# Scoring two blocks of keys during attention instead of during the projections, in a two-layer decoder trunk

## The chip, the cores and the metric

The kernel runs on one core of a Trainium2 chip, as one launch. The metric is the device time of that core in microseconds (us). The time of the kernel before is the median of three runs; one further execution was taken with the hardware profiler.

## The reference, cut to what matters

Two layers over 1024 tokens of width 1024, float32. The change lies in the token mixer of layer 0, a sparse attention: a small "indexer" scores all keys for each query, the 256 best keys that lie before the query are kept, and attention with 16 heads (4 groups) sees only these. `proj` holds q, k, v, the index queries `qi` (8 heads of 64), one index key `ki`, and the 8 head weights `wi`.

```python
def block_fn(args):                      # one block of 128 queries
    qb, qib, wib, start = args
    s = jnp.einsum('bqhd,bsd->bqhs', qib, ki)
    score = jnp.einsum('bqhs,bqh->bqs', jax.nn.relu(s), wib)
    score = jnp.where(causal[None], score, -jnp.inf)
    _, sel = lax.top_k(score, topk)      # topk = 256
    ...
    logits = jnp.where(sel_ok[:, :, None, None, :], logits, -1e30)
    p = jax.nn.softmax(logits, axis=-1)
    o = jnp.einsum('bqgrk,bqkgd->bqgrd', p, vg)
```

After it follow the output projection, a dense FFN, and in layer 1 a short convolution and another FFN; they fill the time from about 640 us to the end and are not touched.

## The kernel before, in words

**A planner writes the order.** The program first records all operations with a due time (`plan.pri`), and `Plan.drain` then plays them through with the costs of `Plan.cost` and issues, for each engine, the ready operation with the earliest due time. So each engine gets a fixed order; an operation with a late due time is pulled forward where the planner finds its engine free. Due times are only an order: attention's run behind the real clock. Block b's attention has due times from `t_att[b]` to `t_att[b+1]`; worked out from lines 829 to 831 `t_att` is 280.6, 287.4, 301.0, 321.4, 348.6, 390.5, 440.7, 499.4 and 566.4 for b = 0 to 8.

**Buffers are rings, in the order in which they are recorded.** `Pool.tile` gives a tile of a ring only after the tile before it has been given, and after all uses of the one `bufs` places back have been issued, whatever the due times are:

```python
if len(ring) > 1:
    plan.link(ring[-2].alloc, al)
if len(ring) > bufs:
    old = ring[-1 - bufs]
    for o in old.ops:
        plan.link(o, al)
```

Two rings matter here: `s4` (SBUF, 3 tiles of 128x1024, shown as `s` in the trace), used by the scoring and by the end of each selection; and `ps_L` (PSUM, 2 tiles), used by every product of `pair_products`: the scoring's and attention's own q k.

**Projections** (`project`). ki is projected first, then the index queries in four steps (half of the tokens, half of the heads), each of two weight tiles (`rope_pair`), rotated and stored to DRAM (`qid`). Then k, q and v.

**Scoring** (`index`). For block b the index queries are loaded back (`karena<-qid`), and for four pairs of heads TensorE multiplies them with the index keys (`ps_L<-karena`, (b+1)*128 columns, at most 512 at a time), ScalarE applies Relu into an `s4` tile, and VectorE multiplies with the head weight and adds (`sc<-s,wiT`). Blocks 0 and 1 need none.

**Counting** (`select`). For a pair of blocks the 256th largest score is found by 31 steps of a binary search on its bits. A step counts, for both blocks, the scores above a threshold, on ScalarE with Sign and an accumulator (pairs 2/3 and 6/7) or on VectorE (pair 4/5) (`junk<-sc,bs`), and then updates the threshold with three small VectorE operations (`bs<-bs`). The due times of the steps go evenly from that of the record to `self.until`. **The end** (`selected`): some ten VectorE passes over `s4` tiles per block, which write `bias`, the mask that attention adds.

**Attention** (`attend`). For each block, group and pair of heads: q k into `ps_L`, mask and maximum on VectorE (`p<-ps_L,bias`), Exp on ScalarE (`p<-p,nm,qsc`), transposes on TensorE, copies to SBUF (`pf<-ps`, ScalarE, or VectorE where the planner finds it free sooner), products with v (`ps_o<-pf,vst`). During blocks 4 and 5 the output projection of the first half (`out_tile`) runs as well. The attention's pools open when the projections' pools (`hp`, `pj`) have been drained.

Of the kernel before, what the change touches and what calls it, by code (L numbers as in the profile page):

```python
# [9 lines left out]
F32 = mybir.dt.float32  # L10
# [40 lines left out]
class Store:  # L51


    def __init__(self, space):
        self.space, self.real, self.parts, self.ops = space, None, {}, []
        self.alloc, self.closed = None, False
# [394 lines left out]
P = 128  # L451
# [3 lines left out]
TB = T // P  # L455
# [6 lines left out]
IH = 8  # L462
TOPK = min(256, T // 4)
FREE_BLK = TOPK // P
# [14 lines left out]
def half_of(h):  # L479
    return slice(h * HW, (h + 1) * HW)  # L480


def blk(b):
    return slice(b * P, (b + 1) * P)
# [313 lines left out]
class Attention:  # L798
# [3 lines left out]
    def __init__(self, tk, w, w_out, ada_w, xspill):  # L802
        self.tk, self.nc, self.w, self.w_out = tk, tk.nc, w, w_out
        self.plan = plan = tk.plan
        self.ada_w, self.xspill = ada_w, xspill

        def dram(name, shape):
            return plan.wrap(plan.tc.dram_tile(shape, F32, name=name), shape)

        self.qd = dram("qd", [HEADS * HD, T])  # L810
        self.qid = dram("qid", [IH * HD, T])
        self.kd = dram("kd", [KVH * HD, T])
        self.rd = dram("rd", [2, 4, 32, T // 4])
        self.kp = Pool(plan, "k4")
        self.keep = keep = Pool(plan, "keep", side="right")
        self.sel = sel = Pool(plan, "sel", side="right")
        self.hp = Pool(plan, "h", side="right")
        self.pj = Pool(plan, "pj", bufs=2, rt=5)
        self.op = Pool(plan, "o", side="right")
        self.at = Pool(plan, "at", bufs=2)  # L820
        self.bias = [keep.tile([P, (b + 1) * P], BF16, name="bias%d" % b) for b in range(TB)]
        self.ssq = keep.tile([P, TB, HEADS], F32, name="ssq")
        self.qsc = keep.tile([P, TB, HEADS], F32, name="qsc")
        self.qsn = keep.tile([P, TB, HEADS], F32, name="qsn")
        self.score = [None] * FREE_BLK + [sel.tile([P, (b + 1) * P], F32, name="sc%d" % b)
                                          for b in range(FREE_BLK, TB)]
        self.bs = sel.tile([P, 4, 16], F32, name="bs")
        self.junk = [sel.tile([P, n], BF16, name="junk%d" % n) for n in (6 * P, T)]
        cum = np.cumsum([0] + [6.8 * (b + 1) for b in range(TB)])
        w = np.array([0.0] * 5 + [41.0 / 26 * (c / 6.8 - 10) for c in cum[5:]])  # L830
        self.t_att = self.T_PROJ + 38 * self.SLOT + cum + w
        self.until = {2: self.t_att[2], 4: self.t_att[4] + 10.0, 6: self.t_att[7]}

    def arena(self, i):

# [75 lines left out]
    def project(self):  # L911
        tk, nc, sp, plan = self.tk, self.nc, self.pj, self.plan
        self.kist = self.arena(0)
        self.ssk = sp.tile([P, TB, KVH], F32, name="ssk", bufs=1)
        self.wiT = sp.tile([P, TB, IH], F32, name="wiT", bufs=1)
        s = 0
        self.unit(s)
        n = HD + IH
        kw = self.s4()
        self.plan.pri = 26.0  # L920
        w = tk.wcols(self.w, C_KI, n)
        for half in range(NH):
            self.unit(s)
            nc.scalar.copy(kw[0:n, half_of(half)], tk.gemm_tile(w, n, self.h[half]))
            s += 1
        self.unit(s + 1)
        self.ki_chain(kw)
        ends = []
        for half, j in ((0, 0), (0, 1), (1, 1), (1, 0)):
            self.unit(s)  # L930
            if (half, j) != (1, 1):
                w = tk.wpair(self.w, C_QI + j * 2 * P)
            ts = slice(max(0, FREE_BLK * P - half * HW), HW)
            ab, sl, e = self.rope_pair(w, half, ts, None, None, s)
            s += (e - s) * (ts.stop - ts.start) / HW
            for two in range(2):
                self.to_dram(ab[two], self.qid, j, two, half, sl)
            if (half, j) == (0, 1):
                ends += self.indexed(s, (2, 3))
        self.free_bias()  # L940
        ends += self.indexed(s, (4, 5, 6, 7))
        for pri, end, args in sorted(ends, key=lambda e: e[0]):
            plan.pri = pri
            end(*args)
        self.unit(s)
        w = tk.wpair(self.w, C_K)
        for half in range(NH):
            ab, sl, s = self.rope_pair(w, half, slice(0, HW), 1, self.ssk, s)
            rk = sp.tile([P, 4, KVH], F32, name="rk", tag="rk")
            tk.rsqrt_small(rk.rearrange("p a b -> p (a b)"),  # L950
                           self.ssk[:, half * 4:half * 4 + 4].rearrange("p a b -> p (a b)"),
                           1.0 / HD, sp.tile([P, 64], F32, name="rst", tag="rst8"))
            self.k_out(ab, rk, half, sl)
        self.load_k()
        for j in range(HEADS // 4):
            self.unit(s)
            w = tk.wpair(self.w, j * 2 * P)
            for half in range(NH):
                ab, sl, s = self.rope_pair(w, half, slice(0, HW), 0,
                                           self.ssq[:, :, 4 * j:4 * j + 4], s)  # L960
                for two in range(2):
                    self.to_dram(ab[two], self.qd, j, two, half, sl)
        self.unit(s)
        tk.rsqrt_small(self.qsc.rearrange("p a b -> p (a b)"),
                       self.ssq.rearrange("p a b -> p (a b)"), 1.0 / HD,
                       sp.tile([P, HW], F32, name="rst", tag="t2"),
                       mult=float(HD ** -0.5))
        nc.vector.tensor_scalar(self.qsn, self.qsc, -1.0, None, op0=ALU.mult)
        w = [tk.weights(tk.cols(self.w[half_of(i)], C_V, KVH * HD)) for i in range(2)]
        for b in range(TB):  # L970
            ps = tk.ps()[:, 0:KVH * HD]
            for k in range(KT):
                hi, lo = (v[:, blk(b % 4)] for v in self.h[b // 4](k))
                tk.mm3(ps, hi, lo, *w[k // 4](k % 4), k == 0, k == KT - 1)
            plan.copy(self.vst.part_of(b)[:, b], ps)
            s += 0.5
            self.unit(s)

    def indexed(self, t, blocks):

# [221 lines left out]
    def attend(self):  # L1202
        tk, nc, plan = self.tk, self.nc, self.plan
        self.o, self.banks, tail = [], 0, None
        self.steps = [(layer, j, i, k) for layer, j in ((0, 2), (0, 3), (0, 4), (0, 5), (1, 0))
                      for i in range(NH) for k in range(KT)]
        for b in range(TB):
            if b % 2 == 0:
                self.o.append([self.op.tile([P, KT, 2 * P], F32R, name="o%s%d" % (v, b),
                                            tag="o" + v, bufs=3) for v in ("hi", "lo")])  # L1210
# [691 lines left out]
```

## Time and profile before

| | us |
|---|---|
| median of 3 runs | 2338.97 (2336.26 to 2341.29) |
| profiled execution, its own time | 2337.17 |
| its span, first to last instruction | 2335.5 |
| TensorE busy in the span | 2259.2 (97%) |
| VectorE, ScalarE busy | 1808.3 (77%), 1115.1 (48%) |

All times in the rows are us from the start of the span. PE is TensorE's matmuls, PEld its weight loads, DVE VectorE, ACT ScalarE, SP the queue that issues the DMAs. In a row of instructions an entry in brackets is the idle time of the engine before it, and what ended it. Every operation is recorded by one helper, so all have the line L244; the tiles tell them apart.

### The profile page before, as it was taken

The numbers are of one execution on the slowest core, as the hardware profiler recorded it, in microseconds if no ns is written. First come the engines' busy times: TensorE is split into PE (matmuls) and PEld (weight loads), VectorE is DVE, ScalarE is ACT, GpSimd is POOL, SyncE is SP. The second block draws the span as 40 slices with busy tenths as digits, with TensorE's granted clock in tenths as the row PEclk, the third lists the DMA queues.
The fourth block names the chain that finished last, engine by engine and source line by source line (L and its number), as shares of the span: only waits on it lengthen the run. The fifth ranks groups of instructions, "written<-read, shape, count | busy, mean of one in ns | idle before, by whom it ended". The sixth has DMA issues, their size and how long they took to land.

```text
span 2335.5 us, 32751 instructions
## 1 busy us (share of the span) xinstructions
PE 2259.2 (97%) x11742; PEld 1827.0 (78%) x11742; DVE 1808.3 (77%) x3697; ACT 1115.1 (48%) x2125; POOL 5.6 (0%) x19
## 2 busy tenths in 40 slices
PE   6999999999999999999999899999999999999999
PEld 6667876877797878888788778878877888887887
DVE  6879999777689886767599899976788655555995
ACT  3576899746655333333344552234553333333443
POOL 0000000000000000000000000000000000000000
PEclk7999999999999999999999999999999999999999
DMA  8423233443344543444845134225344322337443
GB/s 285 136 64 91 90 118 101 140 127 96 109 129 138 182 152 123 151 138 151 302 146 179 57 111 135 82 90 171 104 122 140 91 86 90 100 119 281 141 167 113
DMA packets 305132, 312.30 MB, mean 134 GB/s; under 512 B 15145, under 2 KB 209738, under 8 KB 304970
## 3 DMA queue, kind: packets, MB, share of 16 engines
q1 hardware_dynamic: 303530, 308.91, 41.6%
q8 instruction: 92, 1.51, 0.3%
q10 hardware_dynamic: 1440, 1.31, 0.2%
q14 instruction: 70, 0.57, 0.1%
HBM read 259.05 MB, written 51.12 MB: 133 GB/s over the span
## 4 chain that ended last, share of the span: by engine, by line
PE 71%; DVE 13%; issue 7%; DMA 6%; ACT 3%; POOL 0%; SPq 0%; DVEq 0%; ACTq 0%; POOLq 0%
PE ps_x L244 28%; PE ps_mm L244 19%; PE ps_z L244 15%; PE ps_sm L244 5%; DVE u L244 2%; DVE s L244 2%; PE ps_L L244 2%; PE ps_o L244 2%; DVE wlo L244 2%; DVE v L244 1%; DMA raw<-in_conv_w_in_dram 1%; DVE p L244 1%; DMA raw<-in_ffn_w_up_dram 1%; ACT p L244 1%; DMA raw<-in_ffn_w_gate_dram 1%
## 5 line engine op out<-in xcount | busy, mean ns | idle before, releaser
L244 ACT CAST whi<-s 128x512 fp32r<-128x512 f32 x334 | 206.9, 620 | 449.6 <-DVE s L244 166.5
L244 PE MATMUL ps_x<-t,whi 128*128 128x512 f32 x1088 | 339.0, 392 | 3.8 <-ACT t L244 3.1
L244 ACT CAST whi<-raw 128x512 fp32r<-128x512 f32 (+1 forms) x270 | 165.3, 618 | 337.7 <-PE ps_z L244 133.1
L244 DVE TENSOR_TENSOR wlo<-raw,whi 128x512 fp32r<-128x512 f32 (+1 forms) x276 | 188.2, 685 | 128.0 <-ACT whi L244 126.6
L244 DVE TENSOR_TENSOR wlo<-s,whi 128x512 fp32r<-128x512 f32 x334 | 227.1, 683 | 22.6 <-ACT whi L244 21.9
L244 PEld LDWEIGHTS ps_x<-t,whi 128*128 128x128 f32 x1088 | 204.9, 189 | 47.9 <-ACT t L244 3.5
L244 PE MATMUL ps_x<-t,wlo 128*128 128x512 f32 x544 | 213.4, 392 | 4.4 <-DVE wlo L244 4.4
L244 PE MATMUL ps_x<-h,whi 128*128 128x512 f32 x512 | 158.1, 390 | 0.0
L244 PE MATMUL ps_z<-t,whi 128*128 128x512 f32 x472 | 146.8, 392 | 2.4 <-DVE u L244 2.4
L244 DVE TENSOR_TENSOR s<-raw 128x512 f32<-128x512 f32 x112 | 76.6, 687 | 73.3 <-DMA raw<-in_ffn_w_up_dram 37.7
L244 PE MATMUL ps_x<-ph,whi 128*128 128x512 f32 x396 | 123.7, 391 | 7.2 <-ACT ph L244 7.2
L244 PE MATMUL ps_z<-h,whi 128*128 128x512 f32 x424 | 130.5, 389 | 0.0
L244 PE MATMUL ps_mm<-h,whi 128*128 128x512 f32 x408 | 126.1, 390 | 0.0
L244 ACT ACTIVATE p<-p,nm,qsc 128x128 f32<-128x128 f32 (+7 forms) x128 | 112.2, 879 | 26.6 <-DVE nm L244 21.7
L244 PEld LDWEIGHTS ps_x<-t,wlo 128*128 128x128 f32 x544 | 102.7, 189 | 27.2 <-DVE wlo L244 6.0
L244 DVE SCALAR_TENSOR_TENSOR adacc<-adaw,cact,adacc 128x512 f32<-128x512 f32 x140 | 104.6, 747 | 23.4 <-DMA adaw<-in_ada_w_dram 22.8
L244 DVE CUSTOM_DVE_ANT_0 p<-ps_L,bias 128x512 f32<-128x512 f32 (+3 forms) x192 | 100.0, 551 | 23.6 <-PE ps_mm L244 7.6
L244 ACT ACTIVATE junk<-sc,bs 128x896 bf16<-128x896 f32 (+3 forms) x124 | 109.7, 885 | 15.3 <-DVE bs L244 10.7
L244 PEld LDWEIGHTS ps_x<-h,whi 128*128 128x128 f32 x512 | 95.9, 188 | 19.7
L244 PEld LDWEIGHTS ps_z<-t,whi 128*128 128x128 f32 x472 | 88.9, 189 | 21.6 <-issue 2.2
L244 PE MATMUL ps_x<-h,wlo 128*128 128x512 f32 x256 | 99.9, 390 | 0.0
L244 PE MATMUL ps_mm<-hhi,whi 128*128 128x512 f32 (+2 forms) x240 | 94.4, 394 | 1.6 <-ACT hhi L244 1.6
(364 smaller groups left out, 5299.5 us busy)
## 6 DMA issues: line engine op xcount, KB each, us to landing
ph<-in_ffn_w_down_dram SPq DMA_DIRECT2D x88, 512.0 KB
adaw<-in_ada_w_dram SPq DMA_DIRECT2D x160, 256.0 KB
raw<-in_ffn_w_gate_dram SPq DMA_DIRECT2D x52, 512.0 KB
raw<-in_ffn_w_up_dram SPq DMA_DIRECT2D x52, 512.0 KB
rt<-hid SPq DMA_DIRECT2D x64, 256.0 KB
raw<-in_conv_w_in_dram SPq DMA_DIRECT2D x32, 512.0 KB
hid<-u SPq DMA_DIRECT2D x52, 256.0 KB
raw<-in_ffn_w_down_dram SPq DMA_DIRECT2D x44, 256.0 KB
```

The lines of the kernel that those rows point to most:

```text
L244: f(*[a.get() if isinstance(a, Ref) else a for a in args], **{k: a.get() if isinstance(a, Ref) else a for k, a in kw.items()})
```

## The change

Five things. The index queries of blocks 2 and 3 are scored after the step (1, 1) of the index queries' projection, one step later than before. Blocks 4 and 5 are scored after the last step as before. Blocks 6 and 7 are recorded in `attend` when b is 2, with the due time `t_att[1]`, and their counting runs from there to `t_att[6] - 6` instead of to `t_att[7]`. The ends of 2 to 5 are recorded where all six were; those of 6 and 7 when b is 5. The head weights `wiT` go from the projections' pool to the selection's, which stays open.

```diff
-        self.until = {2: self.t_att[2], 4: self.t_att[4] + 10.0, 6: self.t_att[7]}
+        self.until = {2: self.t_att[2], 4: self.t_att[4] + 10.0, 6: self.t_att[6] - 6.0}
+        self.wiT = sel.tile([P, TB, IH], F32, name="wiT")
...
-        self.wiT = sp.tile([P, TB, IH], F32, name="wiT", bufs=1)
...
-            if (half, j) == (0, 1):
+            if (half, j) == (1, 1):
                 ends += self.indexed(s, (2, 3))
         self.free_bias()
-        ends += self.indexed(s, (4, 5, 6, 7))
-        for pri, end, args in sorted(ends, key=lambda e: e[0]):
-            plan.pri = pri
-            end(*args)
+        ends += self.indexed(s, (4, 5))
+        self.selections(ends)
...
+    def selections(self, ends):
+
+        for pri, end, args in sorted(ends, key=lambda e: e[0]):
+            self.plan.pri = pri
+            end(*args)
...
         for b in range(TB):
+            if b == 2:
+                for i in (6, 7):
+                    plan.pri = self.t_att[1]
+                    self.index(i, i - FREE_BLK)
+                ends = self.select((6, 7), True)
+            if b == 5:
+                self.selections(ends)
             if b % 2 == 0:
```

## Rows read from the trace of the kernel before

**Rows 1.** The page: the span in 40 equal slices, busy tenths of TensorE's matmuls, and its granted clock in tenths of full speed.
```profile
PE   6999999999999999999999899999999999999999
...
PEclk7999999999999999999999999999999999999999
```

**Rows 2.** The view by stages: the stretch in us, its length, busy time of each engine (instructions), granted clock, DMA share, GB/s. The first is the stretch in which blocks 6 and 7 are scored, then the rest of the projections, attention of blocks 0 and 1, of 2 and 3, of 4, of 5.
```profile
core 0: us, PE busy (x) PEld busy (x) DVE busy (x) ACT busy (x) POOL busy (x), PEclk, DMA share, GB/s
161.90:196.00 34.10, 33.36 (x148) 19.02 (x148) 33.65 (x62) 22.33 (x46) 2.36 (x3) 1.00 0.06 17
200.00:312.00 112.00, 110.79 (x634) 97.41 (x633) 105.76 (x378) 96.72 (x205) 0.00 (x0) 0.98 0.43 118
312.00:345.00 33.00, 30.76 (x232) 19.81 (x233) 32.19 (x149) 31.52 (x104) 0.00 (x0) 0.95 0.39 112
345.00:397.00 52.00, 51.55 (x448) 34.13 (x445) 50.66 (x161) 51.24 (x132) 0.00 (x0) 1.00 0.29 85
397.00:455.00 58.00, 55.40 (x486) 43.71 (x487) 44.53 (x167) 48.28 (x101) 0.00 (x0) 1.00 0.43 136
455.00:527.00 72.00, 66.57 (x567) 51.75 (x566) 58.89 (x155) 38.02 (x76) 0.00 (x0) 0.98 0.42 128
```

**Rows 3.** ScalarE in order of time: the first Exp of blocks 0, 2, 4 and 6 (Exp over 128, 384, 640 and 896 keys), which mark where their attention begins.
```profile
314.92 0.49 ACT L244 ACTIVATE p<-p,nm,qsc 128x128 f32<-128x128 f32 x1
345.18 0.74 ACT L244 ACTIVATE p<-p,nm,qsc 128x384 f32<-128x384 f32 x1
399.12 0.93 ACT L244 ACTIVATE p<-p,nm,qsc 128x640 f32<-128x640 f32 x1
527.40 1.13 ACT L244 ACTIVATE p<-p,nm,qsc 128x896 f32<-128x896 f32 x1 [1.01 <-DVE rs L244]
```

**Rows 4.** Scoring of blocks 6 and 7. First the view by stages for the tile karena alone (PE, PEld and ACT busy, clock, DMA share, GB/s); then groups by form: VectorE's accumulations over 1024 and 896 keys and the two first products (count, busy us, mean ns, idle before); then in order of time the first and the last of TensorE's eight groups, and VectorE's last accumulation.
```profile
161.90:196.00 34.10, 15.28 (x64) 5.33 (x64) 0.00 (x0) 1.00 0.06 17
L244 DVE SCALAR_TENSOR_TENSOR sc<-s,wiT,sc 128x1024 f32<-128x1024 f32 x7 | 8.9, 1277 | 0.0
L244 DVE SCALAR_TENSOR_TENSOR sc<-s,wiT,sc 128x896 f32<-128x896 f32 x7 | 8.0, 1146 | 0.1
L244 DVE TENSOR_SCALAR sc<-s,wiT 128x1024 f32<-128x1024 f32 x1 | 0.8, 776 | 0.0
L244 DVE TENSOR_SCALAR sc<-s,wiT 128x896 f32<-128x896 f32 x1 | 0.7, 683 | 0.0
...
162.01 1.77 PE L244 MATMUL ps_L<-karena 64*128 64x512 f32 x8
...
186.20 1.99 PE L244 MATMUL ps_L<-karena 64*128 64x512 f32 x8
193.09 1.28 DVE L244 SCALAR_TENSOR_TENSOR sc<-s,wiT,sc 128x1024 f32<-128x1024 f32 x1
```

**Rows 5.** The view by stages for the counting alone (tile junk): VectorE busy, ScalarE busy, clock, DMA share, GB/s; then, in order of time, the last count of pair 4/5 on VectorE and the last of pair 6/7 on ScalarE.
```profile
200.00:312.00 112.00, 47.42 (x100) 72.35 (x152) 0.98 0.43 118
312.00:397.00 85.00, 5.67 (x12) 8.81 (x15) 0.98 0.33 96
397.00:522.00 125.00, 0.00 (x0) 22.11 (x38) 0.99 0.41 129
353.41 1.00 DVE L244 TENSOR_SCALAR_CACHE_REDUCE junk<-sc,bs 128x768 bf16<-128x768 f32 x1
446.79 1.15 ACT L244 ACTIVATE junk<-sc,bs 128x1024 bf16<-128x1024 f32 x1
```

**Rows 6.** The ends of selections (tile s in attention): the view by stages (PE, PEld, DVE, ACT busy, clock, DMA share, GB/s), and the last of these operations, block 7's mask.
```profile
312.00:345.00 33.00, 0.00 (x0) 0.00 (x0) 6.40 (x11) 0.00 (x0) 0.95 0.39 112
345.00:397.00 52.00, 0.00 (x0) 0.00 (x0) 11.06 (x14) 0.00 (x0) 1.00 0.29 85
496.66 1.22 DVE L244 SCALAR_TENSOR_TENSOR bias<-s,s 128x1024 bf16<-128x1024 f32 x1
```

**Rows 7.** The index queries' way through DRAM: SP's queue in order of time; what it waited for (us, times, longest); TensorE in order of time; and the view by stages of the stretch after TensorE's wait.
```profile
119.19 3.02 SPq L244 DMA_DIRECT2D raw<-in_attn_w_in_dram  x2
123.23 1.92 SPq L244 DMA_DIRECT2D qid<-rt  x2
132.11 2.02 SPq L244 DMA_DIRECT2D karena<-qid  x4
...
SPq L244 <- DMA qid<-rt: 9.6, 2, 6.8
...
135.11 2.50 PE L244 MATMUL ps_L<-karena 64*128 64x512 f32 x8 [4.60 <-DMA karena<-qid]
135.00:141.00 6.00, 5.89 (x18) 3.60 (x19) 2.33 (x4) 3.08 (x8) 0.00 (x0) 0.50 0.33 92
```

**Rows 8.** Block 5's attention in order of time: VectorE's prefix sum in block 7's end of selection, and TensorE's two waits behind it.
```profile
482.79 2.29 DVE L244 TENSOR_TENSOR_SCAN s<-s 128x1024 f32<-128x1024 f32 x1
486.14 0.70 PE L244 MATMUL ps_L<-karena,qst 64*128 64x256 f32 x4 [1.48 <-DVE mx L244]
489.16 1.79 PE L244 MATMUL ps_L<-karena,qst 64*128 64x512 f32 x4 [2.32 <-DVE mx L244]
```

**Rows 9.** ScalarE's activation tables, in order of time: the load before the indexer's stage and the one at attention's start.
```profile
85.44 1.28 ACT L244 ACT_TABLE_LOAD   x1
313.62 1.28 ACT L244 ACT_TABLE_LOAD   x1
```

## The prediction, made before the changed kernel was run

> **What bounds the kernel now.** I read the page first: TensorE is busy in nearly every slice and its clock is nearly always granted [rows 1]. Then the view by stages [rows 2], which is the one to dwell on. In the stretch where blocks 6 and 7 are scored, TensorE is busy 33.36 of 34.10 us and VectorE 33.65; in the rest of the projections TensorE 110.79 of 112, while ScalarE has 15 us free. In attention of blocks 0 to 3 (312 to 397) three engines are full at once: VectorE 82.85 of 85, ScalarE 82.75, TensorE's matmul row 82.3, but its weight loads only 53.9. There the two elementwise engines set the pace and TensorE's row is stretched. From block 4 on the output projection fills TensorE (122 of 130 in blocks 4 and 5), and ScalarE has 43.7 us free, VectorE 26.6. So the change takes work out of a stage that TensorE bounds and puts it into one that ScalarE and VectorE bound. Borders between blocks come from the first Exps [rows 3]: block 2 begins at 345, block 4 at 399, block 6 at 527, each well behind its due time.
>
> The sum is made against the profiled execution (2337.17; 2335.5 of span and 1.7 around it). The median of the runs is 1.8 above it, and I carry the difference over to the median.
>
> **Step 1: the projections lose the scoring of 6 and 7.** Its eight groups of matmuls keep TensorE busy 15.3 us [rows 4]. TensorE was waiting for nothing else there [rows 2], so attention starts earlier by that. Bounds: 13, if VectorE's work at the end is not through earlier, and 17, with what changing between two shapes of matmul costs. I take **-15.3**. Leaving with it are 18.4 us of VectorE (14 accumulations, 8.9 + 8.0, and two first products, 0.8 + 0.7) and the counting of 18 steps on ScalarE that lay in 200 to 312 (some 40 of the 72.35 us [rows 5]); these were hidden behind TensorE there, and gain nothing.
>
> **Step 2: the same scoring as a stage of attention.** Two rings say when it runs. Its `s4` tiles follow those of the ends of 4 and 5, so it can't begin before block 4's end; and block 2's first q k takes its `ps_L` tile behind the scoring's sixteen. So attention of 2 can't begin until the scoring's products are through, and these are held by three `s4` tiles, that is by VectorE's accumulations: 18.4 us, of which the last three (3.8) run when TensorE has gone on. That makes 14.6 us in which attention's own q k stands. What is queued behind is all of block 2's chain: mask, Exp, transposes, products with v. Bounds: 7, if half of it lies behind what ScalarE still has of block 1; and 26, the 162.01 to 188.2 that it took before, when VectorE had other work [rows 4]. I take **+14.6**, nearer to the middle, since blocks 0 and 1 leave both engines full too (32.2 and 31.5 of 33 [rows 2]).
>
> **Step 3: the counting of 6 and 7.** Its due times now go from 287.4 to 434.7 in 30 parts of 4.9; 13 of the 31 steps are due before block 4's 348.6. Before, 4 steps ran in 312 to 397, for 8.81 us of ScalarE, 2.2 each [rows 5]. Nine more are 19.8 us; first counts, scaling and small operations some 6 of VectorE. What leaves this stage: the last three steps of pair 4/5 (5.7 us [rows 5]) and the ends of 4 and 5 (11.1 [rows 6]), which step 2 needs earlier. Net 9 us more over two engines that are 97% busy and can trade the copies `pf`, `rw`, `on`: 9 / 2 / 0.97 = **+4.6**. Bounds 0 (steps slip to blocks 4 and 5) and +10 (nothing can be traded).
>
> **Step 4: blocks 0 and 1.** The ends of 2 and 3 (6.4 us of VectorE [rows 6]) go into the projections, where VectorE has lost 18.4 us of scoring in a stage that is 15.3 shorter; the ends of 4 and 5 come into their place. (11.1 - 6.4) / 2 is 2.3; a part fits ahead of attention, I take **+1**, bounds -3 and +5.
>
> **Step 5: blocks 4 and 5.** 18 steps instead of 9, 20 us more of ScalarE on 86 of 130. TensorE still sets the pace, but waits in order for a busier engine: **+1**, bounds -5 (the waits of 1.48 and 2.32 us behind block 7's prefix sum [rows 8] might not come again) and +6.
>
> **Step 6: the queries of 2 and 3 one step later.** Before, TensorE stood 4.60 us for the load of block 4's index queries, and its clock was 0.50 for the next 6 us [rows 7], 7.6 in all. SP had waited 6.8 us for the two stores of the last step, issued at 123.23 behind 1 MB of weights. The stores, that load and their order are the same after the change; blocks 2 and 3 no longer need theirs there, which TensorE didn't wait for. What is scored before the load lands is work that the planner had already found for that time. **0**; bounds -7.6 and 0.
>
> **Edits at nothing.** `wiT` in another pool moves no work. Relu between Exps is not in the trace: one table load served the indexer's stage with its Relus and Signs, one served attention with Signs between the Exps [rows 9, 5]. Bounds 0, and 41 us if each of 16 groups of Relus needed two loads of 1.28; I take 0, by Sign, which ran under both. The Trainium skill (ScalarE: Activation LUTs, "Table sets: the hidden batching unit") says that cheap functions such as relu are in every set, by which nothing is loaded either; no row here shows it for Relu.
>
> **Sum:** -15.3 + 14.6 + 4.6 + 1 + 1 + 0 = +5.9; 2343.1 on the profiled execution, **2345** on the median.
>
> **Where a page weighs in.** By TensorE's busy row alone (51.55 of 52 us in blocks 2 and 3 [rows 2]) TensorE would bound attention too, the scoring would add its 15.3 there, and steps 2 to 5 would shrink to that: 0 in all. The weight loads of that stage fill 34 of 52 us, against 97 of 112 in the projections, and I go by these. The Trainium skill (Perfetto Trace Analysis, "Identifying the Most-Contended Engine") says the same of the two rows: matmul busy is no good measure, the share of weight loads is.
>
> **The rivals.**
> *Forecast (0.62):* the work changes place and costs slightly more where it goes; own range 2338 to 2354. Somewhat under half of it lies within 0.2% (4.7 us, about what a measurement of this kernel can tell from no change).
> *Hidden after all (0.26), faster:* scoring needs VectorE most, blocks 0 and 1 ScalarE; run against each other, only half of step 2 shows (-7.6), and the counting slips into the 43.7 us that ScalarE has free in blocks 4 and 5 (-4.6): 2345 - 12.2 = 2333; with step 6's 7.6 as well 2325. For it: in [rows 2] the free time is there. Against it: the rings put scoring between the blocks, not beside them, and due times put 13 steps ahead of block 4.
> *Block 6 waits for its mask (0.12), much slower:* before, counting ended at 446.79 and block 7's mask stood at 496.66, 31 us ahead of block 6's first Exp at 527.40 [rows 3, 5, 6]. Now attention begins at about 297, scoring ends at about 343, and 31 steps must end some 15 us ahead of 533. That allows 5.5 us a step. Before, as filler in blocks 4 and 5, a step took about 5.3 (9.5 steps in some 50 us). It is more urgent now, so I expect 4 to 4.5 and no wait; at 6 a step block 6 waits 10 us, at 6.5 25: about 2360.
> *The change doesn't do what it says:* scoring can't stay in the projections, since its rings come after the ends of 2 to 5; it can only come later than described. That is part of the last rival.
>
> **How the numbers follow.** Time: 2345. Low end: the second case without step 6's gain, and a part of its tail, 2329; high end: the forecast's upper end and the near part of the third, 2356. Left out are about 0.1 on each side. Slower by over 0.2%: 0.33 of the forecast and 0.12, 0.45; within: 0.29 of the forecast, 0.29; faster 0.26.
>
> **What the changed profile would show.** Step 1: first Exp at 297 to 302. Step 2: the tile karena alone (no qst) on TensorE between the q k of blocks 1 and 2, Relus on ScalarE there, and the first Exp of block 2 within 5 us of its 345. Steps 3 and 4: first Exp of block 4 at 400 to 406. Step 5: that of block 6 at 529 to 536, with the last Sign before 515. Step 6: a wait of 4 to 5 us for karena<-qid still there. I am wrong if attention of block 4 begins before 395 (hidden), or if TensorE stands before block 6. Nothing after 660 should differ but by the shift.

## The result and the profile after

The changed kernel takes 2365.78 us (median of 4 runs, 2365.06 to 2367.40), the kernel before 2340.13 beside it: a ratio of 1.0117, with a 95% interval of 1.0103 to 1.0130. That is slower, and beyond the upper end of the range (2356). The profiled execution took 2367.40, 30.2 more than the one before, and its span grew by the same 30.2, from 2335.5 to 2365.7.

The page after, in the form of [rows 1]: TensorE's matmuls and its clock. The two slices with 7 and 8 (the sixth and seventh, 296 to 414 us) were 9 before.

```profile
PE   6999978999999999999999998999999999999999
...
PEclk7999998999999999999999999999999999999999
```

ScalarE in order of time, as [rows 3]: the table load and the first Exp of block 0, the last Exp of block 1, the first Exps of blocks 2, 4 and 6.

```profile
292.28 1.28 ACT L244 ACT_TABLE_LOAD   x1
293.58 0.49 ACT L244 ACTIVATE p<-p,nm,qsc 128x128 f32<-128x128 f32 x1
...
320.37 0.62 ACT L244 ACTIVATE p<-p,nm,qsc 128x256 f32<-128x256 f32 x1
...
356.68 0.71 ACT L244 ACTIVATE p<-p,nm,qsc 128x384 f32<-128x384 f32 x1 [5.04 <-DVE nm L244]
...
419.05 0.95 ACT L244 ACTIVATE p<-p,nm,qsc 128x640 f32<-128x640 f32 x1
...
558.79 1.14 ACT L244 ACTIVATE p<-p,nm,qsc 128x896 f32<-128x896 f32 x1 [0.45 <-DVE nm L244]
```

Attention begins 21.3 us earlier than in [rows 3] and block 2 begins 11.5 later: 36 us pass between block 1's last Exp and block 2's first, and before, the one followed the other. The same in lengths, from first Exp to first Exp, in us; the four columns on the right are experiments that follow:

| | before | after | scoring back | quarter of scoring | narrow counting | both cut |
|---|---|---|---|---|---|---|
| first Exp of block 0 | 314.9 | 293.6 | 321.7 | 291.6 | 296.3 | 296.6 |
| block 0 | 14.1 | 13.0 | 16.1 | 13.7 | 12.9 | 14.9 |
| block 1 and the border to 2 | 16.1 | 50.1 | 16.8 | 33.5 | 51.0 | 33.4 |
| blocks 2 and 3 | 53.9 | 62.4 | 56.7 | 62.3 | 51.3 | 51.2 |
| blocks 4 and 5 | 128.3 | 139.7 | 126.1 | 141.4 | 131.9 | 129.9 |
| block 6 to the last Exp | 99.2 | 95.6 | 99.0 | 100.1 | 99.0 | 99.3 |
| span | 2335.5 | 2365.7 | 2345.9 | 2355.5 | 2350.4 | 2337.5 |

After minus before, line by line and before rounding: -21.3, -1.1, +33.9, +8.4, +11.5, -3.7, and +2.5 for all that follows; sum +30.2. Each column is one execution. In eleven profiles (the changed kernel and ten of the experiments) TensorE, VectorE and ScalarE run the same instructions in the same order up to 290 us, and still the first Exp lies between 290.8 and 297.2. So a difference of a few us between two columns in the first line shows nothing by itself.

The view by stages after, as [rows 2]: the stretch of the projections in which 6 and 7 were scored before; the projections after it; blocks 0 and 1; the two halves of the border; blocks 2 and 3; 4; 5.

```profile
core 0: us, PE busy (x) PEld busy (x) DVE busy (x) ACT busy (x) POOL busy (x), PEclk, DMA share, GB/s
161.90:196.00 34.10, 34.10 (x180) 29.20 (x179) 33.36 (x102) 14.28 (x32) 0.00 (x0) 1.00 0.40 105
200.00:290.00 90.00, 90.00 (x533) 80.02 (x532) 86.91 (x286) 50.26 (x121) 0.00 (x0) 1.00 0.39 111
293.00:320.00 27.00, 25.13 (x186) 15.55 (x186) 26.78 (x123) 26.43 (x91) 0.00 (x0) 0.94 0.51 153
320.00:334.00 14.00, 8.27 (x61) 4.98 (x59) 13.83 (x26) 7.20 (x20) 0.00 (x0) 0.88 0.00 0
334.00:357.00 23.00, 16.19 (x60) 5.27 (x60) 20.67 (x27) 13.59 (x28) 1.14 (x2) 0.90 0.00 1
357.00:419.00 62.00, 54.45 (x380) 33.08 (x382) 43.64 (x173) 59.05 (x135) 0.00 (x0) 0.89 0.21 60
419.00:487.00 68.00, 61.95 (x543) 49.28 (x544) 51.00 (x181) 58.20 (x123) 0.00 (x0) 0.99 0.40 125
487.00:559.00 72.00, 68.22 (x601) 55.84 (x599) 62.88 (x178) 48.84 (x96) 0.00 (x0) 1.00 0.38 114
```

Three things are to be seen. In the projections ScalarE is now nearly half idle (50.26 of 90). At the border (320 to 357) TensorE's matmuls are busy 24.5 of 37 us and ScalarE 20.8. In blocks 2 and 3 ScalarE is full (59.05 of 62) while VectorE has 18 us free; before, both were full [rows 2].

The border itself. First VectorE: the masks with which the ends of 4 and 5 close, the first accumulation after them, and the last one; then one of block 2's masks, the counting's first pass over block 7's scores, and `nm`, for which block 2's first Exp waits. Then TensorE: scoring's groups with their waits, the last row being block 2's own q k.

```profile
324.20 0.82 DVE L244 SCALAR_TENSOR_TENSOR bias<-s,s 128x640 bf16<-128x640 f32 x1
332.08 0.96 DVE L244 SCALAR_TENSOR_TENSOR bias<-s,s 128x768 bf16<-128x768 f32 x1
332.96 1.15 DVE L244 SCALAR_TENSOR_TENSOR sc<-s,wiT,sc 128x896 f32<-128x896 f32 x1
...
353.20 1.28 DVE L244 SCALAR_TENSOR_TENSOR sc<-s,wiT,sc 128x1024 f32<-128x1024 f32 x1
354.40 0.55 DVE L244 CUSTOM_DVE_ANT_0 p<-ps_L,bias 128x384 f32<-128x384 f32 x1
...
355.35 1.22 DVE L244 TENSOR_SCALAR_CACHE_REDUCE junk<-sc 128x1024 bf16<-128x1024 f32 x1
...
356.49 0.16 DVE L244 TENSOR_TENSOR nm<-mx,qsn 128x2 f32<-128x2 f32 x1
...
328.73 3.36 PE L244 MATMUL ps_L<-karena 64*128 64x512 f32 x8 [3.51 <-ACT s L244]
334.27 5.19 PE L244 MATMUL ps_L<-karena 64*128 64x512 f32 x16 [2.19 <-ACT s L244]
...
347.94 2.11 PE L244 MATMUL ps_L<-karena 64*128 64x512 f32 x8 [1.34 <-ACT s L244]
350.71 0.59 PE L244 MATMUL ps_L<-karena,qst 64*128 64x384 f32 x2 [0.67 <-ACT s L244]
```

The waits of 320 to 357 (us in total, times, longest):

```profile
PEld ps_L L244 <- ACT s L244: 19.3, 15, 3.8
PE ps_L L244 <- ACT s L244: 8.6, 7, 3.5
ACT p L244 <- DVE nm L244: 5.0, 1, 5.0
ACT s L244 <- DVE bias L244: 4.1, 1, 4.1
```

So the border has three parts in a row: to 334 the ends of 4 and 5 (scoring's Relu waits 4.1 us for a mask, which frees its `s4` tile, and TensorE waits for the Relu); to 351 the scoring, TensorE waiting for a Relu at nearly every group; and to 357 attention's chain starting again (Exp waits 5.0 us, since block 2's mask passes lie on VectorE among the last accumulations and the counting's first pass). In the first two parts nothing of attention runs beside it, except the tail of block 1 in the first.

The counting by stage (VectorE busy, ScalarE busy, clock, DMA share, GB/s), as [rows 5]:

```profile
160.00:296.00 136.00, 54.97 (x116) 37.35 (x98) 0.99 0.41 115
296.00:357.00 61.00, 7.14 (x16) 0.00 (x0) 0.92 0.18 53
357.00:419.00 62.00, 0.00 (x0) 28.57 (x48) 0.89 0.21 60
419.00:559.00 140.00, 0.00 (x0) 45.07 (x76) 0.99 0.39 119
```

The tile `s` in the first part of the border (PE, PEld, VectorE, ScalarE busy, then as above), as [rows 6]; of VectorE's 12.02 us some 1.7 are scoring's first two passes, the rest the ends of 4 and 5:

```profile
320.00:334.00 14.00, 0.00 (x0) 0.00 (x0) 12.02 (x16) 2.93 (x6) 0.88 0.00 0
```

### The profile page after: what moved, and what is told of

Same layout as the page of the kernel before. It is cut to its first block, busy times and chain, and to the rows that moved or that the text cites. A ratio compares the mean times of both kernels' runs of the same rounds, so it can differ in the third digit from the quotient of the medians.

```text
span 2365.7 us, 32740 instructions
## 1 busy us (share of the span) xinstructions
PE 2268.1 (96%) x11742; PEld 1831.4 (77%) x11742; DVE 1825.7 (77%) x3723; ACT 1104.5 (47%) x2099; POOL 4.5 (0%) x19
## 4 chain that ended last, share of the span: by engine, by line
PE 66%; issue 15%; DVE 10%; DMA 5%; ACT 3%; SPq 0%; POOL 0%; DVEq 0%; ACTq 0%; POOLq 0%
PE ps_x L244 27%; PE ps_mm L244 15%; PE ps_z L244 15%; PE ps_sm L244 5%; PE ps_L L244 2%; DVE u L244 2%; PE ps_o L244 2%; DVE s L244 2%; DVE wlo L244 1%; DVE v L244 1%; ACT junk L244 1%; DMA raw<-in_ffn_w_up_dram 1%; DMA raw<-in_ffn_w_gate_dram 1%; DMA raw<-in_conv_w_in_dram 1%; ACT p L244 1%
## 5 line engine op out<-in xcount | busy, mean ns | idle before, releaser
L244 ACT CAST whi<-raw 128x512 fp32r<-128x512 f32 (+1 forms) x264 | 162.1, 618 | 338.8 <-PE ps_z L244 134.5
L244 ACT ACTIVATE junk<-sc,bs 128x384 bf16<-128x384 f32 (+1 forms) x124 | 109.5, 883 | 23.1 <-DVE bs L244 21.4
L244 DVE CUSTOM_DVE_ANT_0 p<-ps_L,bias 128x512 f32<-128x512 f32 (+3 forms) x192 | 100.3, 552 | 21.3 <-PE ps_mm L244 9.5
L244 PEld LDWEIGHTS ps_x<-h,whi 128*128 128x128 f32 x512 | 95.9, 188 | 19.8
L244 PE MATMUL ps_L<-karena,qst 64*128 64x512 f32 (+3 forms) x384 | 89.4, 553 | 7.4 <-DVE mx L244 6.4
```

Of the source, the lines that this page charges most:

```text
L244: f(*[a.get() if isinstance(a, Ref) else a for a in args], **{k: a.get() if isinstance(a, Ref) else a for k, a in kw.items()})
```

## The experiments

Each run is compared with the kernel before on the same chip; 0.1% is 2.3 us. "Block n begins" is its first Exp in the profiled execution.

**The shift of 2 and 3 alone.** The kernel before with one line of the change:

```diff
-            if (half, j) == (0, 1):
+            if (half, j) == (1, 1):
                 ends += self.indexed(s, (2, 3))
```

> The kernel before with only the scoring of blocks 2 and 3 moved behind the step (1, 1). Theory as predicted: 0, TensorE still waits 4 to 5 us for the index queries of block 4; 2338 to 2342. Rival: this move is worth the 6 us by which the changed kernel's attention began earlier than the 15.3 of step 1, attention begins at 306 to 308 and the time is 2332 to 2335.

Ratio 0.9993 (0.9981 to 1.0005), 2339.96. In the whole time it costs and brings nothing. In its profile attention began at 319.1, 4.2 us later than before, which the whole time doesn't show.

**Everything but the place.** The changed kernel, with scoring and counting of 6 and 7 recorded in the projections again:

```diff
-        ends += self.indexed(s, (4, 5))
-        self.selections(ends)
+        ends += self.indexed(s, (4, 5, 6, 7))
+        self.late, ends = ends[4:], ends[:4]
+        self.selections(ends)
...
-            if b == 2:
-                ...
             if b == 5:
-                self.selections(ends)
+                self.selections(self.late)
```

> The changed kernel, with the scoring and the record of the counting of 6 and 7 back behind those of 4 and 5 in the projections; all else of the change stays (2 and 3 a step later, counting due until t_att[6] - 6, ends of 6 and 7 recorded at block 5, wiT in the other pool). Theory (the place of the scoring is the whole loss): within 0.2% of before, 2337 to 2346, first Exp at 313 to 319. Rival (due times or the later record of the ends cost part of it): 2349 or more.

Ratio 1.0009 (0.9997 to 1.0021), 2343.43: no difference from before that the runs can tell. The place of the scoring, with what hangs on it, is the whole loss. The first Exp came at 321.7, a little later than I had expected.

**Counting due later.** The changed kernel with the old end of the counting:

```diff
-        self.until = {..., 6: self.t_att[6] - 6.0}
+        self.until = {..., 6: self.t_att[7]}
```

> The changed kernel with one number put back: the counting of 6 and 7 is due by t_att[7] (499) again instead of t_att[6] - 6 (434.7), 7.1 a step instead of 4.9. Theory: blocks 2 and 3 take 68 us instead of 54 since the counting comes ahead of Exp on ScalarE at 3.7 us a step (17 steps there); with the later due time fewer steps lie there, block 4 begins some 8 to 12 us earlier than its 425, and the time is 2354 to 2358 unless block 6 then waits for its mask. Rival: blocks 2 and 3 are slow for another reason (VectorE's ends, a colder clock); then block 4 begins where it does now and the time stays at 2366.

Ratio 1.0104 (1.0074 to 1.0134), 2364.27. Block 4 began 9.4 us earlier than in the changed kernel (409.61 for 419.05; the 425 and the 68 us of the expectation are not what the profile of the changed kernel has), block 5 19.1 earlier (468.6), block 6 only 7.3. Attention itself had begun 2.8 us earlier in this profile. VectorE's mask of block 6, then ScalarE's first Exp of block 6:

```profile
546.62 1.09 DVE L244 SCALAR_TENSOR_TENSOR bias<-s,s 128x896 bf16<-128x896 f32 x1
...
551.45 1.13 ACT L244 ACTIVATE p<-p,nm,qsc 128x896 f32<-128x896 f32 x1 [6.51 <-DVE nm L244]
```

The mask is finished 3.7 us ahead of the Exp, which waited 6.5. So counting that gets out of the way of blocks 2 to 5 comes back as a wait of block 6. In the changed kernel the mask was written at 537.63, 21 us ahead.

**Another ring for the scoring's tiles.** The Relu tiles of 6 and 7 from attention's ring `p`, so that scoring needn't wait for the ends of 4 and 5:

```diff
-            rs = [self.s4()[:, 0:wd] for _ in range(2)]
+            rs = [(self.s5() if b > 5 else self.s4())[:, 0:wd] for _ in range(2)]
```

> The changed kernel, but the Relu tiles of blocks 6 and 7 come from attention's ring p (4 tiles) instead of s4. Theory: of the 36 us between the q k of blocks 1 and 2 some 14 go into waiting for the s4 tiles of the ends of 4 and 5; without that wait block 2's first q k comes at 338 to 343 instead of 351 and the time is 2354 to 2360. Rival: VectorE is the bound of the whole stretch (ends and accumulations together, 31 us), the order does not matter, block 2 begins within 3 us of 351 and the time is 2363 to 2368.

Ratio 1.0099 (1.0075 to 1.0123), 2363.99; block 2 began at 351.1, 5.6 us earlier. Scoring started earlier, but the mask of block 5 then came at 357.8 instead of 332.1, behind it. The time is in the rival's range, though block 2's begin moved further than the rival's 3 us.

**The ends earlier.** The counting of 2/3 and 4/5 due earlier:

```diff
-        self.until = {2: self.t_att[2], 4: self.t_att[4] + 10.0, ...}
+        self.until = {2: self.t_att[0] - 6.0, 4: self.t_att[0], ...}
```

> The changed kernel with the counting of 2 to 5 due by t_att[0] - 6 and t_att[0] (274.6 and 280.6) instead of 301 and 358.6, so that the ends of 4 and 5 are not due after block 2's attention, which their s4 tiles hold up. Theory: these ends run before attention or in block 0, block 2 begins 10 to 14 us earlier than 351, and the time is 2353 to 2358. Rival: VectorE has no room for them in the projections (19 of 20 us busy there), so projections or blocks 0 and 1 grow by what the stage loses; 2363 to 2368.

Ratio 1.0107 (1.0085 to 1.0129), 2366.22, as the rival says. The mask of 5 was there at 312.8, 19.3 us earlier, but attention began 6.9 us later (300.5), block 1 13.1 later (319.8), and block 2 at 361.6. What the border got shorter, the projections and block 0 got longer.

From these three my theory was that VectorE, nearly full from 140 to 355, sets the length of all of it, and that ScalarE is the next limit. The next runs test that.

**VectorE relieved in the projections.** Counting of 4/5 on ScalarE as well:

```diff
-    ON_ACT, IDX = (2, 3, 6, 7), 0.5
+    ON_ACT, IDX = (2, 3, 4, 5, 6, 7), 0.5
```

> The changed kernel, with the counting of pair 4/5 on ScalarE too, instead of VectorE. Theory (VectorE has no free time from 140 to 355, so everything that it must do ahead of block 2 adds up): VectorE loses some 54 us of counting between 160 and 320, ScalarE had 62 us free from 160 to 296 and takes it. The ends of 4 and 5 lie ahead of attention or in block 0, block 2's first Exp comes 12 to 17 us earlier than 356.7 (340 to 345), block 4's at 403 to 409; time 2350 to 2356. Rival (the stage is long because of its own chain of load, TensorE, Relu, accumulation through two rings): block 2 begins no earlier than 352, time 2361 to 2366.

Ratio 1.0134 (1.0107 to 1.0160), 2375.31. VectorE's share of 200 to 290 fell to 60.38 of 90 us and ScalarE's rose to 81.87; yet attention began 4.9 us later and block 2 at 368.4, 11.7 later. The theory expected 12 to 17 earlier: it falls. The time is beyond the rival's range too. Taking VectorE's counting away made nothing earlier, but ScalarE got it instead and was nearly full with it, so the run doesn't show what VectorE alone would have been worth, nor why the border grew to 55.4 us. The same with the counting of 6/7 due until `t_att[6] + 25`:

> The changed kernel, with the counting of pair 4/5 on ScalarE and that of 6/7 due until 31 us later (t_att[6] + 25 instead of - 6). Theory (two limits behind each other, VectorE ahead of block 2, then ScalarE in blocks 2 to 5): with the first one lifted the scoring ends at about 340, so the later due times don't make the mask of block 6 late as they did alone; block 4's first Exp at 397 to 403, block 6's below 535, time 2340 to 2349. Rival (block 6 waits for its mask again): mask of 6 at 545 or later, time 2358 to 2366.

Ratio 1.0135 (1.0109 to 1.0162), 2374.72, with block 6's mask at 563.5 instead of 537.6. The mask is as late as the rival said, but the time is beyond both ranges.

**VectorE relieved in the stage.**

```diff
-                else:
+                elif b < 6:
                     nc.vector.scalar_tensor_tensor(sc, r, wi, sc, op0=ALU.mult, op1=ALU.add)
```

> The changed kernel, with 14 of the 16 multiply-and-adds by which VectorE accumulates the scores of blocks 6 and 7 left out (only the first head counts); TensorE's products and the Relus are all there. Theory (VectorE sets the length of the stage): 16.9 us of VectorE go, block 2's first Exp comes 13 to 17 us earlier than 356.7 (340 to 344), time 2350 to 2356, the rest given back by the later blocks. Rival (rings and TensorE/ScalarE set it): their 15.5 us stay in line behind the ends of 4 and 5, block 2 comes at most 5 us earlier, time 2361 to 2366.

Ratio 1.0059 (1.0040 to 1.0078), 2357.09. Block 2 began at 353.65, 3.0 us earlier, as the rival says; the time lies between the two ranges. Three Signs of the counting, about 1.2 us of ScalarE each, had got in ahead of that Exp, so without them the stage would be some 6 or 7 us shorter (an estimate), still far from the theory's 13 to 17. TensorE, then ScalarE, in it:

```profile
342.71 2.11 PE L244 MATMUL ps_L<-karena 64*128 64x512 f32 x8 [0.39 <-ACT s L244]
345.09 2.11 PE L244 MATMUL ps_L<-karena 64*128 64x512 f32 x8 [0.27 <-ACT s L244]
...
341.57 2.06 ACT L244 ACTIVATE s<-ps_L 128x512 f32<-128x512 f32 x4 [0.52 <-PE ps_L L244]
343.95 2.06 ACT L244 ACTIVATE s<-ps_L 128x512 f32<-128x512 f32 x4 [0.31 <-PE ps_L L244]
```

Two `ps_L` tiles take 2.1 us of TensorE (1.77 for the first group of [rows 4]), 2.06 of ScalarE and, where it is there, 2.3 to 2.6 of VectorE (two accumulations of [rows 4]): three engines of nearly the same pace, handing tiles to each other. Taking one away leaves the other two. More of the kernel's gain came later: the counting began 11.8 us earlier (first Sign at 347.2 instead of 359.0), and block 6 began 10.4 earlier.

**The counting made cheaper.** The same 31 steps over a quarter of the keys of 6 and 7:

```diff
+        q = 4 if pair[0] == 6 else 1
...
-                    nc.scalar.activation(junk[i], scs[i], AF.Sign, ...
+                    nc.scalar.activation(junk[i][:, 0:wds[i] // q], scs[i][:, 0:wds[i] // q], AF.Sign, ...
```

> The changed kernel, with the 31 counting steps of pair 6/7 over a quarter of the keys only (224 and 256 of 896 and 1024); number of steps, small operations and due times stay. Theory (ScalarE is full from 357 to 440 by the counting ahead of the Exps): a step costs ScalarE some 1.2 us less, 17 of them lie in 357 to 424; block 2 begins at 357 as before, block 4's first Exp comes 10 to 18 us earlier than 419.1 (401 to 409), and since the mask of block 6 comes earlier too block 6 follows; time 2347 to 2356. Rival (blocks 2 to 5 are long for another reason): block 4 at 415 to 419, time 2361 to 2366.

Ratio 1.0027 (1.0013 to 1.0041), 2350.79: 0.9% less than the changed kernel. Of the counting's ScalarE time in blocks 2 to 5, 73.6 us, 37.2 were left. In the table above, blocks 2 and 3 fall from 62.4 to 51.3 and blocks 4 and 5 from 139.7 to 131.9; the border stays. Block 4's first Exp, at 411.5, lies between the two cases of the expectation; the time is the theory's.

**The scoring spread out.** If the stage is dear since attention has nothing beside it, pieces of it between the pairs of attention should be cheaper (one pair of heads ahead of every second pair, here in blocks 1 and 2):

```diff
-            if b == 2:
-                ...
+            if b == self.FIRST:
+                heads = iter([v for i in (6, 7)
+                              for v in [self.scored(i, i - FREE_BLK, self.s5)] * (IH // 2)])
...
+                    if b in (self.FIRST, self.FIRST + 1) and pr:
+                        next(next(heads))
```

> The changed kernel, with the scoring of 6 and 7 not recorded in one piece between blocks 1 and 2, but one pair of heads at a time ahead of every second pair of attention in blocks 1 and 2, with its Relu tiles from attention's p ring. Same instructions. Theory (in one piece the scoring is a stage of its own: both rings hand everything to it, and TensorE, ScalarE and VectorE wait for each other tile by tile with no attention beside it): no hole, block 4's first Exp at 400 to 410 instead of 419.1, time 2346 to 2356. Rival (VectorE and ScalarE are full in blocks 0 to 3 anyway, the sum counts and not the order): block 4 at 415 to 420, time 2360 to 2367.

Ratio 1.0162 (1.0146 to 1.0178), 2380.31: slower than the changed kernel (1.0117), and block 4 began at 429.3. Both cases of the expectation miss. With the later due time, and with the pieces in blocks 0 and 1:

> The spread form (scoring of 6 and 7 one pair of heads at a time through blocks 1 and 2) with the counting of 6/7 due until t_att[7], as in the kernel before. Theory (stage of its own, then ScalarE full by counting): both reliefs add, since the scores are there earlier: block 4 at 392 to 402, mask of block 6 at or before 540, time 2340 to 2350. Rival (block 6 waits for its mask, as with the later due time alone): mask of 6 at 545 or later, time 2355 to 2364.

> As the spread form with the later due time, but the pieces lie in blocks 0 and 1 instead of 1 and 2. Theory (stage of its own, and the counting wants to begin early): scores done by about 335, block 4 at 395 to 405, mask of 6 before 530, time 2338 to 2348. Rival (blocks 0 and 1 leave both engines full, so the 18 us of VectorE lengthen them one for one, and block 6 waits): time 2352 to 2364.

1.0175 (1.0159 to 1.0192), 2383.29, and 1.0169 (1.0146 to 1.0192), 2382.84, slower than either case had it; the masks of block 6 came at 568.6 and 567.8. Since these forms take scoring's tiles from attention's ring `p`, one more leaves that ring alone (`FIRST = 2`, `self.s4` for `self.s5`):

> The changed kernel, with the scoring recorded one pair of heads at a time ahead of every second pair of attention in blocks 2 and 3, with its Relu tiles from the s4 ring as in the change; attention's p ring is left alone, unlike in the spread forms before. Theory P (those were slow since scoring took half of attention's four p tiles): first Exp of block 2 at 325 to 335, of block 4 at 385 to 405, time 2345 to 2358. Theory Q (engines run their instructions in order, so a piece of scoring ahead of a pair makes attention's chain stand wherever it lies): block 4 at 412 or later, time 2362 to 2385.

Ratio 1.0143 (1.0113 to 1.0173), 2377.40; time and block 4 are as theory Q says. Block 2 began at 319.1, but block 4 at 413.0. The view by stages of its blocks 2 and 3, and the two largest waits of attention there:

```profile
319.00:368.00 49.00, 37.77 (x260) 21.57 (x258) 35.71 (x89) 31.93 (x85) 0.29 (x1) 0.93 0.08 22
368.00:413.00 45.00, 38.41 (x275) 22.41 (x272) 37.54 (x97) 32.48 (x75) 0.29 (x1) 0.92 0.29 84
...
PEld ps_L L244 <- DVE mx L244: 17.1, 8, 5.7
PE ps_L L244 <- DVE mx L244: 13.4, 7, 5.1
```

94 us for two blocks that took 53.9, with no engine full: TensorE 81% busy, VectorE 78%, ScalarE 69%. TensorE stands 13.4 us in seven waits for a mask on VectorE; in order, a piece of scoring on one engine holds up attention on the next. But the scoring itself lies in these 94 us. From block 1's first Exp to block 4's it is 108.4 us here and 112.4 in the changed kernel, and block 4 begins 6.0 us earlier. So the loss against the changed kernel lies behind: the counting began only at 407.9 (3.40 us of it ran in blocks 2 and 3 instead of 28.57, then 70.06 in blocks 4 and 5 instead of 45.07), blocks 4 and 5 took 158.9 us instead of 139.7, and block 6's first Exp had to wait:

```profile
571.90 1.13 ACT L244 ACTIVATE p<-p,nm,qsc 128x896 f32<-128x896 f32 x1 [19.93 <-DVE nm L244]
```

In the other three spread forms it waited 8.6 to 13.5 us, and the first Sign came at 366.9 to 390.7, against 359.0 in the changed kernel. So no run here shows that the scoring in pieces is dearer in itself; later counting goes with it each time.

**Two prices that add.** Three quarters of the scoring left out, alone and with the narrow counting:

```diff
-        for hp in range(IH // 2):
+        for hp in range(IH // 2 if b < 6 else 1):
```

> The changed kernel, with three of the four pairs of heads left out of the scoring of blocks 6 and 7 (12 of 16 tiles on TensorE, their Relus and their accumulations); counting and all else stay. Theory (the loss is the whole stage plus the counting behind it, each at its own price): three quarters of a stage of 18 to 20 us go, block 2's first Exp comes 13 to 17 us earlier than 356.7 (340 to 344), time 2348 to 2354. Rival (the border between blocks 1 and 2 is long for the order alone: ends of 4 and 5, refilling of attention's chain): block 2 at 350 or later, time 2360 or more.

> The changed kernel, with a quarter of the scoring of 6 and 7 (as in the run before) and their counting over a quarter of the keys (as in the run with the narrow counting, which alone took 15). Theory (two prices that add): 13 to 17 less by the one, some 15 by the other, time 2333 to 2340, first Exp of block 4 at 388 to 397. Rival (both relieve the same wait, or a third limit stands behind them): 2345 or more.

Alone: ratio 1.0065 (1.0045 to 1.0085), 2359.48; block 2 began at 338.8, 17.9 us earlier, more than the theory expected, but the time fell by 0.52% only and lies between the two cases. Both: 0.9959 (0.9944 to 0.9974), 2334.48, as the theory says, and faster than before. Against the changed kernel the scoring's cut takes 0.52%, the counting's 0.90%, both together 1.58% (of the kernel before), which is their sum within the intervals. In the table each cut moves its own lines and leaves the other's within 2 us: 50.1 to 33.5 at the border by the one, blocks 2 to 5 by the other.

No version that does the whole work was faster than before; those with the scoring in the projections were equal to it.

## Why the prediction was wrong

The mechanism was the one forecast (the work changes place and costs more where it goes), and the sign was the likeliest of the three. The size was not: +30.2 on the profiled execution where the sum said +5.9.

**Step 1 (-15.3) measured -21.3** as the shift of the first Exp, beyond its bound of 17; against the run with the scoring put back it is 28.1. Much of the spread of first Exps is there before the projections' wait of step 6. Counted from the first scoring group behind that wait, attention begins 162.7 to 164.9 us later in the eleven profiles with equal projections, and 189.9 us later in both runs that shift 2 and 3 but score 6 and 7 in the projections. So the place of the scoring is worth 25 to 27 us there. Before the change it is 179.8 us, but 22 more of the projections' matmuls (`ps_mm`, 447 for 425, some 5 us by 0.24 each) had run ahead of that wait; so the move of 2 and 3 took about 5 us of the gain back at attention's start (an estimate), though the whole time of its run doesn't show it.

The step took TensorE's matmul row for full in [rows 2], priced its 15.3 busy us, and said that TensorE was waiting for nothing else there. That reading was wrong. Weight loads filled only 19.02 of those 34.10 us and VectorE 33.65, and the scoring's weight loads waited for Relus (the kernel before, 161.9 to 196; us in total, times, longest):

```profile
PEld ps_L L244 <- ACT s L244: 5.4, 13, 0.8
```

In the run with the scoring put back it is plainer. The view of the stretch of its scoring, and what TensorE's matmuls waited for there:

```profile
156.00:206.00 50.00, 45.78 (x192) 27.46 (x192) 49.07 (x108) 31.48 (x66) 1.33 (x3) 0.93 0.14 39
PE ps_mm L244 <- DVE wlo L244: 3.1, 2, 2.6
```

By the measure that I used for attention, VectorE set the pace there and not TensorE; no run takes VectorE's work alone out of that stage, so this is argued and not shown. After the change the same stretch as in [rows 2] has 29.20 us of weight loads. The Trainium skill (Perfetto Trace Analysis, "Identifying the Most-Contended Engine") calls matmul occupancy no good measure of how close TensorE is to its limit; the traces agree here, and I applied it to one stage only.

**Step 2 (+14.6, bounds 7 and 26): the border grew by 33.9.** The run with a quarter of the scoring gives 16.6 for three quarters of it, so about 22 for all (an estimate in proportion). That is inside the bounds, but the argument for the lower value (the last accumulations run when TensorE has gone on) was wrong: block 2's first masks queue on VectorE among those accumulations and the counting's first pass, and Exp waits 5.0 us.

**Step 4 (+1) is the term that was missing.** Block 0 changed by -1.1, but the ends of 4 and 5 arrived at the border with next to nothing beside them: most of VectorE's 12.02 of 14 us above, where [rows 6] have 11.06 spread over 52, and scoring, held by the same ring, stood behind. With 22 for the scoring, 12 of the 33.9 us are left for the ends and for the restart of attention's chain. No run leaves the ends out, so their own share is by subtraction. I had taken these 11.1 us off blocks 2 and 3 in step 3, where they shortened nothing, and charged 1 where they went. Steps 2 and 4 together said +15.6 for blocks 0 and 1 and the border; they took +32.8.

**Step 3 (+4.6) measured +8.4.** Its work was right: 28.57 us of counting against 8.81, the 19.8 that were predicted. Its division by two engines was wrong. This program counts 6 and 7 on ScalarE alone, and the two engines did not trade enough: ScalarE 59.05 of 62, VectorE 43.64. With narrow counting the 8.4 are gone (51.3). Whether better costs in the planner would move more copies to VectorE I didn't try.

**Step 5 (+1, up to 6) measured +11.5**, given back in part by block 6 on (-3.7). 45.07 us of counting lay there instead of 22.11; the 43.7 us that ScalarE had free in the sum of two blocks were no cover for 23 more: in block 4 it is now busy 58.20 of 68. Narrow counting took 7.9 of it away.

**Step 6 (0) was right for the whole time**, though not at attention's start (step 1). The shift alone gave 0.9993, and the wait is still there, 4.69 us where it was 4.60 [rows 7]:

```profile
130.85 2.50 PE L244 MATMUL ps_L<-karena 64*128 64x512 f32 x8 [4.69 <-DMA karena<-qid]
```

**Edits at nothing were right.** 32 Relus ran between Exps (323 to 351), and ScalarE loaded no table between the load at 292.28 above and this one, after attention:

```profile
674.47 1.28 ACT L244 ACT_TABLE_LOAD   x1
```

The Trainium skill (ScalarE: Activation LUTs, "Table sets: the hidden batching unit") has relu in every set; the trace agrees, as these Relus needed no load of their own.

**The rivals.** "Hidden after all" fell: nothing ran beside the scoring. "Block 6 waits for its mask" did not happen (mask at 537.63, Exp at 558.79); with the later due time, which left blocks 2 and 3 shorter, it did. Of the markers, the karena groups between blocks 1 and 2 and the remaining wait came as said; the first Exp (293.6 for 297 to 302), block 2 (356.7 for 340 to 350), block 4 (419.1 for 400 to 406), block 6 (558.8 for 529 to 536) and the last Sign (518.7, not before 515) did not.

**What stays open:** why block 6 to its last Exp took 3.7 us less, which engine's relief brought the projections more than 15.3 us, and what the lower clock cost (below).

## What to carry to other kernels

Where a piece of work goes between two stages and takes its tiles from their rings, price the whole chain at its new place (what the rings force ahead of it, its own length, and the refilling of the stage behind it), because nothing runs beside it; what it leaves behind is priced by the engine that sets the pace there, and a full matmul row doesn't say which that is. Work that the program gives to one engine is charged to that engine alone, not spread over those that are busy beside it. And cutting each of two suspected costs alone and both together tells whether they add; taking away one engine of a chain of three equals tells little.

## What the runs showed that I had not expected

Spreading the scoring didn't make the kernel faster. Three of the four spread forms were 0.45 to 0.6% slower than the scoring in one piece, and the fourth 0.26% slower, which the intervals don't separate. The Trainium skill (Perfetto Trace Analysis, "Optimization Strategy") says that interleaving regimes with different contended engines may improve performance; no run here shows a gain from it, and none shows that the pieces by themselves cost more, since the counting behind them began later each time.

The granted clock was lower at the new place. It was 0.88 and 0.90 at the border, where blocks 0 and 1 have 0.95 in [rows 2], and 0.89 in blocks 2 and 3, which have 1.00 there. In blocks 0 and 1 of the run with the counting of 4/5 on ScalarE it was 0.61:

```profile
298.00:320.00 22.00, 19.89 (x94) 11.41 (x96) 15.45 (x73) 18.15 (x62) 0.00 (x0) 0.61 0.52 156
```

The prediction had no term for it, and no run here separates its price from that of the waits around it. With narrow counting the clock was 0.93 from 360 to 412, and blocks 2 and 3 took 51.3 us, less than the 53.9 before at 1.00: there, a clock below 1.00 alone did not make the stage long.
